# Attention's filler held behind marks of three engines, w_out's loads ordered behind the old sums' loads, heads written in their gate's place

## The chip, the cores and the metric

The kernel runs on one core of one Trainium2 chip. The metric is the device time of one execution in microseconds (us), and lower is better. The core has four compute engines, each with its own queue of instructions: TensorE (PE, matmuls), VectorE (DVE), ScalarE (ACT) and GpSimd (POOL). SyncE (SP) computes nothing here: it issues nearly all DMA transfers, one behind the other. An engine that waits holds up everything behind the waiting instruction in its queue, and that holds for SP too.

## The reference, cut to what matters

One layer of a hybrid decoder: one projection, three groups of heads (attention, a state-space mixer, a gated recurrence), a gate on each, and one output projection. The change touches the attention and the output projection alone.

```
def fox_attention(q, k, v, log_f, q_g, k_g):          # 8 heads x 64, 2048 tokens, causal
    q = rms_norm(q, q_g);  k = rms_norm(k, k_g)
    c = jnp.cumsum(log_f.astype(jnp.float32), axis=1)
    ...
        logits = jnp.einsum('bhqd,bhkd->bhqk', q_i, kt) * scale + (c_i[..., :, None] - ck[:, :, None, :])
        logits = jnp.where(kpos[None, :] <= qpos[:, None], logits, -jnp.inf)
        p = jax.nn.softmax(logits.astype(jnp.float32), axis=-1)
        return jnp.einsum('bhqk,bhkd->bhqd', p, vt)

        y_att = fox_attention(...) * jax.nn.silu(z_att)
        ...
        mix = jnp.concatenate([y_att, y_ssd, y_lru], axis=-1)      # 512 + 1024 + 512 columns
        h = h + jnp.einsum('bse,ed->bsd', mix, w_out[l])           # w_out is 2048 x 1024
```

## The kernel before, in words

**Stages.** Projections, the state-space mixer and the recurrence take the time up to 1267 us, attention the stretch from 1267 to 1866 us, and a tail of output projection alone the rest, up to 2023 us. The order of the instructions on every engine is fixed when the program is built: a scheduler takes the instructions as the code gives them, and places them by its own estimate of when each is ready. What runs on the chip is that order, with waits where one engine needs another's result.

**Attention.** There are 64 units, eight heads by eight blocks of 256 queries, numbered j; a unit has one to eight tasks (j, kp), each of 256 keys, 288 tasks in all and 36 in a head. A task is a score (`score`: four matmuls at L1006 and L1007 into the PSUM tile T), two exponentials on ACT (L1017 writes ph, the high part, and L1018 overwrites T), a subtraction on DVE (L1019, pl, the low part), a sum of rows on POOL (L1028 and L1031), and three tasks later the product with v (`av`, L1061 and L1063, into the tile O). `maxima` prepares the unit that comes next: its row maxima (L965 on PE, L970 to L975 on DVE), and the loads of queries (`load_q`, L820 to L822), of the gate `za` (L950), and at each head's middle unit of the next head's keys and values (`load_head`, L805 to L809). `finish` ends a unit: ACT copies half of O into `to` (L1075), DVE adds the other parts (L1077, L1078), POOL multiplies by za into `to` (L1079), and SP stores `to` in DRAM (L1085).

**The filler.** Between the tasks stands the output projection, which needs nothing of attention until its last quarter. `sweeps` is a generator that goes over w_out's sixteen blocks of 128 rows in four sweeps of four: rows 12 to 15, then 8 to 11, then 4 to 7 and 0 to 3 mixed. Its partial sums go through DRAM between sweeps (`pt_d`: loads `xr` at L1179 and `xo` at L1215, stores at L1190). Each half tile takes twelve matmuls (L1139 to L1141) and two additions on DVE. A sweep needs the next one's eight blocks of w_out in two parts: `load_wo` loads a block as `wor` (SP, L840), and splits it into `woh` (ACT, L854 or L858) and `wol` (DVE, L855 or L859). A load is issued one block ahead of the split that needs it, and there are eight splits for each sweep. `mix` loads the inputs of a tile (`mt`) and makes their high part `mh` on ACT (L1126) and low part `ml` on POOL (L1127).

**What sets the filler's place.** `fill` runs after each task and takes the filler one step on. Its `issue_after` adds a rule to what the step issues: an instruction *on the mark's engine* must stand behind the mark, with no wait on the chip. The mark before is one score matmul, LAG = 4 tasks back, so that only the filler's PE instructions are held. Its ACT, DVE, POOL and SP instructions stand wherever the scheduler's estimate puts them.

Of the kernel before, what the change touches and what calls it, by code (L numbers as in the profile page):

```python
# [18 lines left out]
P = 128  # L19
# [16 lines left out]
LAG = 4  # L36
# [14 lines left out]
def hybrid_block(ctx, tc, x, norm_g, w_in, q_norm_g, k_norm_g, forget_b, ssd_conv_w, ssd_conv_b,  # L51
# [772 lines left out]

    def load_wo(ws, k0, half, last):
        pl = [(k0 + i, n) for i in range(4) for n in range(2)]
        tags = [f"u{p}{half}_{k}" for k in range(KD) for p in "hl"]
        raw = {}  # L830

        def load(j):
            k, n = pl[j]
            if j + 1 < len(pl):
                raw[j] = [upa.tile([P, 512], F32, name=f"wor{k}_{n}", tag=tags[2 * j + 3])]
            else:
                raw[j] = last(f"wor{k}_{n}")
            m = 512 // len(raw[j])
            for i, r in enumerate(raw[j]):
                dma(r, w_out[k * P:(k + 1) * P, n * 512 + i * m:n * 512 + (i + 1) * m])  # L840

        load(0)
        yield
        for j, (k, n) in enumerate(pl):
            if j + 1 < len(pl):
                load(j + 1)
            h = upa.tile([P, 512], F32R, name=f"woh{k}_{n}", tag=tags[2 * j])
            l = upa.tile([P, 512], F32R, name=f"wol{k}_{n}", tag=tags[2 * j + 1])
            m = 512 // len(raw[j])
            for i, r in enumerate(raw[j]):  # L850
                hc, lc = h[:, i * m:(i + 1) * m], l[:, i * m:(i + 1) * m]
                if 4 <= k < 12:
                    g = c1("sg", k - 4)
                    A.activation(hc, r, AF.Copy, scale=g)  # L854
                    V.scalar_tensor_tensor(lc, r, g, hc.bitcast(F32), op0=ALU.mult,  # L855
                                           op1=ALU.subtract)
                else:
                    A.copy(hc, r)  # L858
                    V.tensor_tensor(lc, r, hc.bitcast(F32), op=ALU.subtract)  # L859
            ws[k, n] = (h, l)  # L860
            yield
# [72 lines left out]
        G.memset(mz, 0.0)  # L934
    U = [{} for _ in units]

    def maxima(j):


# [4 lines left out]
        def first():  # L944
            if j % 2 and j + 1 < len(units):
                load_q(j + 1)
            za = a4.tile([64, 256], F32, name=f"za{j}", tag="za")
            u["za"] = za
            p, b = divmod(h, 2)
            dma(za, za_d[p][b * 64:b * 64 + 64, sb * 256:(sb + 1) * 256])  # L950
            if j % 8 == 4 and h < 7:
                load_head(h + 1)
# [39 lines left out]
    def score(j, kp):  # L992
# [21 lines left out]
                flip(j + 1, pt[:, 384:512])  # L1014
        ph = a5.tile([P, 512], F32R, name=f"ph{j}_{kp}", tag="ph")
        pl = a5.tile([P, 512], F32R, name=f"pl{j}_{kp}", tag="pl")
        A.activation(ph[:, 0:n], pt[:, 0:n], AF.Exp, scale=-1.0)  # L1017
        A.activation(pt[:, 0:n], pt[:, 0:n], AF.Exp, scale=-1.0)  # L1018
        V.tensor_tensor(pl[:, 0:n], pt[:, 0:n], ph[:, 0:n].bitcast(F32), op=ALU.subtract)  # L1019
        u[kp] = ph, pl  # L1020

        e = ph.bitcast(F32)
# [43 lines left out]
    def finish(j):  # L1066
# [3 lines left out]
        po = u["O"]  # L1070
        T.matmul(po[0:65, 256:512], onr, u["ah"], start=False, stop=False, skip_group_check=True)
        T.matmul(po[0:65, 256:512], onr, u["al"], start=False, stop=True, skip_group_check=True)
        to = a3.tile([64, 256], F32, name=f"to{j}", tag="to")
        su = a3.tile([1, 256], F32, name=f"su{j}", tag="su")
        A.copy(to, po[64:128, 0:256])  # L1075
        A.copy(su, po[64:65, 256:512])
        V.tensor_tensor(to, po[0:64, 0:256], to, op=ALU.add)  # L1077
        V.tensor_tensor(to, po[0:64, 256:512], to, op=ALU.add)  # L1078
        G.tensor_tensor(to, to, u["za"], op=ALU.mult)  # L1079
        p, b = divmod(h, 2)  # L1080
        cs = slice(sb * 256, (sb + 1) * 256)
        qt = slice(sb * 2, sb * 2 + 2)

        def store():
            dma(at_d[p][b * 64:b * 64 + 64, cs], to)  # L1085
            dma(s_d[qt, h:h + 1, :].rearrange("i o t -> o i t"),
                su.rearrange("o (i t) -> o i t", i=2))
            if h < 7:
                return

            sr = a1.tile([16, P], F32, name=f"sr{j}", tag="sr")
            dma(sr, s_d[qt].rearrange("i h t -> (i h) t"))
            V.reciprocal(sr, sr)
            dma(r_d[qt].rearrange("i h t -> (i h) t"), sr)
            later(lambda: ready.add(sb), 4)
# [71 lines left out]
    def wo_last(nm):  # L1167
        return [o4.tile([P, 512], F32, name=nm, tag="xr")]

    def sweeps():  # L1170
        for i in range(2):
            more = load_wo(ws[i + 1], SEQ[i + 1][0], 1 - i, wo_last)
            xrs = {}

            def load_xr(j):
                t, n = divmod(j, 2)
                if t < NT:
                    xrs[j] = o4.tile([P, 512], F32, name=f"xr{t}_{n}_{i}", tag="xr")
                    dma(xrs[j], (pt_d if i else xf)[t * P:(t + 1) * P, n * 512:n * 512 + 512])  # L1179

            load_xr(0)
            cur = mix(0, *SEQ[i])
# [16 lines left out]
            for _ in more:  # L1199
                pass  # L1200

        more = load_wo(ws[3], SEQ[3][0], 1, wo_last)
        xs = {}
        work = [(t, 2) for t in range(LEAD)]
        for t in range(NT):
# [5 lines left out]
        for w, (t, i) in enumerate(work):  # L1211
            tsl = slice(t * P, (t + 1) * P)
            if i == 2:
                xs[t] = o3.tile([P, D], F32, name=f"xo{t}", tag="xo")
                dma(xs[t], pt_d[tsl, :])  # L1215
            if i == 3 and cur is None:
                while t // 2 not in ready:
                    yield True
# [21 lines left out]
                next(filler)  # L1240
        flip(0, psS.tile([P, P], F32, name="pm0", tag="S"))
    count = [0, FIRST]
    recent = []

    def fill(ins):
        count[0] += 1
        recent.append(ins)
        want = FIRST + count[0] * RATE // 288 + MORE * max(0, count[0] - 288 + END)
        while want > count[1]:
            with tc.issue_after(recent[max(0, len(recent) - 1 - LAG)].ins):  # L1250
                if next(filler):
                    break
            count[1] += 1
# [60 lines left out]
```

## Time and profile before

| | |
|---|---|
| runs | 2018.38, 2027.57 and 2033.65 us, median 2027.57 |
| the profiled execution: its own time | 2024.83 us |
| its span, from the first to the last instruction | 2023.1 us |
| mean granted clock of TensorE | 0.99 |
| PE busy in the span | 1953.6 us (97%) |
| DVE, ACT, POOL busy in the span | 1302.0, 1005.7 and 803.6 us |

How to read it: PE is busy nearly all the time, so a change to the work of the other engines can shorten the time only by PE's idle stretches and by the time that PE runs at half its clock. A row of a timeline gives the start, the duration, the engine, the line, the operation with out<-in, and in brackets the idle time of that engine ahead of it and what ended it. PEclk is the granted clock as a share of 2.4 GHz; 0.50 is 1.2 GHz.

### The profile page before, as it was taken

How to read it: one execution, taken by the hardware profiler on the slowest of the kernel's cores; microseconds unless marked ns; L12 is line 12 of the kernel's file. 1: busy time of each engine (PE TensorE's matmuls, PEld its weight loads, DVE VectorE, ACT ScalarE, POOL GpSimd, SP SyncE). 2: the span in 40 equal slices, each digit the busy share in tenths (PEclk: the TensorE clock that was granted, in tenths of full speed). 3: DMA queues.
4: the chain of work that ended last, by engine and by line, in shares of the span. 5: the costliest groups of instructions: out<-in, count | busy, mean ns of one | idle time of the engine just before them, and what ended most of it. 6: DMA issues, size and time to landing. Idle time of an engine off the chain costs nothing.

```text
span 2023.1 us, 34947 instructions
## 1 busy us (share of the span) xinstructions
PE 1953.6 (97%) x11941; PEld 1708.9 (84%) x11941; DVE 1302.0 (64%) x2573; ACT 1005.7 (50%) x2174; POOL 803.6 (40%) x920
## 2 busy tenths in 40 slices
PE   7999999999999999989999999999999999998899
PEld 6898888898989899778887897888888988887787
DVE  6748555574645556768577535678778887887333
ACT  6624444453544444544444333576766776765010
POOL 0100000232222324444564201687878887876110
PEclk9999999999999999999999999999999999999999
DMA  5332223121212145667666725664663664704453
GB/s 190 82 100 65 70 74 105 47 64 43 70 37 74 32 120 148 183 170 204 211 187 177 192 80 182 189 182 127 186 180 121 181 170 126 217 28 131 125 172 125
DMA packets 260034, 261.32 MB, mean 129 GB/s; under 512 B 26724, under 2 KB 198016, under 8 KB 258304
## 3 DMA queue, kind: packets, MB, share of 16 engines
q1 hardware_dynamic: 259696, 259.05, 43.7%
q8 instruction: 95, 1.56, 0.3%
q0 software_dynamic: 160, 0.03, 0.1%
q14 instruction: 83, 0.68, 0.1%
HBM read 164.22 MB, written 94.77 MB: 128 GB/s over the span
## 4 chain that ended last, share of the span: by engine, by line
PE 42%; DMA 6%; DVE 3%; ACT 2%; issue 2%; POOL 1%; SPq 0%; DVEq 0%; POOLq 0%; ACTq 0%
PE po L1139 5%; PE po L1140 5%; PE po L1141 5%; PE T L1006 3%; PE T L1007 3%; PE O L1061 3%; PE S L965 3%; PE O L1063 2%; DMA ab<-acs_d 2%; PE pza L360 1%; PE pza L361 1%; PE pza L359 1%; PE py L698 1%; PE pqk L347 1%; PE pqk L343 1%
## 5 line engine op out<-in xcount | busy, mean ns | idle before, releaser
L1139 PE MATMUL po<-woh,mh 128*128 128x512 f32 x512 | 204.9, 400 | 11.9 <-DVE xo L1145 7.6
L1019 DVE TENSOR_TENSOR pl<-T,ph 128x512 fp32r<-128x512 f32 (+1 forms) x288 | 187.2, 654 | 45.3 <-ACT T L1018 43.4
L1140 PE MATMUL po<-wol,mh 128*128 128x512 f32 x512 | 202.2, 395 | 0.0
L1141 PE MATMUL po<-woh,ml 128*128 128x512 f32 x512 | 201.4, 395 | 0.0
L1017 ACT ACTIVATE ph<-T 128x512 fp32r<-128x512 f32 (+1 forms) x288 | 165.2, 574 | 55.7 <-PE T L1007 49.9
L1031 POOL TENSOR_TENSOR ac<-ac,ph 128x512 f32<-128x512 f32 x120 | 155.6, 1296 | 29.7 <-ACT ph L1017 24.2
L1018 ACT ACTIVATE T<-T 128x512 f32<-128x512 f32 (+1 forms) x288 | 164.7, 572 | 0.1
L359 PE MATMUL pxx<-uh,wh 128*128 128x512 f32 x384 | 153.3, 401 | 2.2 <-ACT uh L304 2.1
L1006 PE MATMUL T<-q,k 128*128 128x256 f32 x576 | 148.0, 281 | 6.1 <-DVE pl L1019 2.6
L360 PE MATMUL pxx<-ul,wh 128*128 128x512 f32 x384 | 153.7, 401 | 0.0
L1061 PE MATMUL O<-ph,vv 128*128 128x256 f32 (+1 forms) x576 | 149.5, 279 | 3.5 <-DVE to L1078 2.9
L361 PE MATMUL pxx<-uh,wl 128*128 128x512 f32 x384 | 151.2, 396 | 0.0
L347 PE MATMUL pqk<-wh,ul 128*128 128x256 f32 x512 | 150.9, 295 | 0.0
L343 PE MATMUL pqk<-wh,uh 128*128 128x256 f32 x512 | 148.4, 290 | 0.0
L345 PE MATMUL pqk<-wl,uh 128*128 128x256 f32 x512 | 148.3, 290 | 0.0
L420 DVE SCALAR_TENSOR_TENSOR accx<-rtx,cv,accx 128x512 f32<-128x512 f32 x144 | 108.1, 752 | 59.3 <-ACT accx L417 56.3
L1007 PE MATMUL T<-qx,kx 128*128 128x256 f32 x576 | 144.4, 282 | 0.0
L345 PE MATMUL pzs<-wl,uh 128*128 128x256 f32 x512 | 143.7, 281 | 0.0
L347 PE MATMUL pzs<-wh,ul 128*128 128x256 f32 x512 | 143.3, 280 | 0.0
L1063 PE MATMUL O<-pl,vv 128*65 128x256 f32 x576 | 143.2, 280 | 0.0
L343 PE MATMUL pzs<-wh,uh 128*128 128x256 f32 x512 | 143.0, 281 | 0.0
L975 DVE TENSOR_REDUCE mc<-S 128x1 f32<-128x512 f32 x192 | 128.8, 682 | 21.2 <-PE S L965 19.3
(357 smaller groups left out, 5702.3 us busy)
## 6 DMA issues: line engine op xcount, KB each, us to landing
ab<-acs_d SPq DMA_DIRECT2D x64, 256.0 KB
pt_d<-xr SPq DMA_DIRECT2D x64, 256.0 KB
wr<-in_w_in_dram SPq DMA_DIRECT2D x112, 128.0 KB
xt<-in_x_dram SPq DMA_DIRECT2D x16, 512.0 KB
xs_d<-stx SPq DMA_DIRECT2D x32, 256.0 KB
v_d<-vs SPq DMA_DIRECT2D x32, 256.0 KB
wr<-in_w_in_dram SPq DMA_DIRECT2D x128, 64.0 KB
zs_d<-zs SPq DMA_DIRECT2D x32, 256.0 KB
```

What stands on the lines that cost most here:

```text
L343: T.matmul(ps[:, i, :], h[k][:, sl], wh[k], start=(k == 0 and i == 0), stop=False, skip_group_check=True)
L345: T.matmul(ps[:, i, :], h[k][:, sl], wl[k], start=False, stop=False, skip_group_check=True)
L347: ins = T.matmul(ps[:, i, :], l[k][:, sl], wh[k], start=False, stop=last, skip_group_check=True)
L360: T.matmul(ps, wh[k][:, ms], ul[tb][k], start=False, stop=False)
L1006: T.matmul(ps, k2[:, ks], q3[:, qs], start=(jj == 0), stop=False, skip_group_check=True)
L1007: ins = T.matmul(ps, kx[:, ks], qx[:, qs], start=False, stop=True, skip_group_check=True)
L1019: V.tensor_tensor(pl[:, 0:n], pt[:, 0:n], ph[:, 0:n].bitcast(F32), op=ALU.subtract)
L1061: T.matmul(po[:, qs], vv[:, kt, 0:128], ph[:, cs], start=(kt == 0), stop=(kt == 2 * sb + 1), skip_group_check=True)
L1063: T.matmul(po[0:65, q2], vv[:, kt, 64:129], pl[:, cs], start=False, stop=False, skip_group_check=True)
L1139: T.matmul(ps, mh[:, j, :], h, start=(j == 0), stop=False)
L1140: T.matmul(ps, mh[:, j, :], l, start=False, stop=False)
L1141: T.matmul(ps, ml[:, j, :], h, start=False, stop=(j == 3))
```

## The change

Three edits, all in attention and its filler.

1. **Marks of three engines.** `score` notes the exponential of each task (ACT, L1017) and the subtraction (DVE, L1019); `fill` notes the score matmul as before. Each filler step is held behind all three, four tasks back. The filler's ACT and DVE instructions are held now as its matmuls were. POOL and SP are not.
2. **w_out's loads.** `load_wo` gets a list of the loads of the old sums, `loads`; each load of a block of w_out for sweeps 1, 2 and 3 is ordered on SP's queue behind the last load of old sums known when it is issued (order only, no wait).
3. **The heads' place.** The product with the gate is written into `za` itself, not into `to`, and stored from there. `za` has five buffers (four before), `to` two (three before). So the load of za(j+5) overwrites what the store of unit j reads, and has to wait for that store's landing; before, the load of za(j+4) had to wait only for POOL's product of unit j. `to` is free once POOL has read it; before, only once its store had landed.

```
-    def load_wo(ws, k0, half, last):
+    def load_wo(ws, k0, half, last, behind=()):
...
-                dma(r, w_out[k * P:(k + 1) * P, n * 512 + i * m:n * 512 + (i + 1) * m])
+                put = dma(r, w_out[k * P:(k + 1) * P, n * 512 + i * m:n * 512 + (i + 1) * m])
+                if behind:
+                    tc.add_manual_dep(put.ins, behind[-1].ins.name, mybir.DependencyInfo(
+                        mybir.DependencyClass.NoSync, mybir.DependencyReason.DATA))
...
+    marks = {"P": [], "A": [], "V": []}
...
-            za = a4.tile([64, 256], F32, name=f"za{j}", tag="za")
+            za = a5.tile([64, 256], F32, name=f"za{j}", tag="za")
...
-        A.activation(ph[:, 0:n], pt[:, 0:n], AF.Exp, scale=-1.0)
+        marks["A"].append(A.activation(ph[:, 0:n], pt[:, 0:n], AF.Exp, scale=-1.0))
...
-        V.tensor_tensor(pl[:, 0:n], pt[:, 0:n], ph[:, 0:n].bitcast(F32), op=ALU.subtract)
+        marks["V"].append(V.tensor_tensor(pl[:, 0:n], pt[:, 0:n], ph[:, 0:n].bitcast(F32),
+                                          op=ALU.subtract))
...
-        to = a3.tile([64, 256], F32, name=f"to{j}", tag="to")
+        to = a2.tile([64, 256], F32, name=f"to{j}", tag="to")
...
-        G.tensor_tensor(to, to, u["za"], op=ALU.mult)
+        G.tensor_tensor(u["za"], to, u["za"], op=ALU.mult)
...
-            dma(at_d[p][b * 64:b * 64 + 64, cs], to)
+            dma(at_d[p][b * 64:b * 64 + 64, cs], u["za"])
...
-            more = load_wo(ws[i + 1], SEQ[i + 1][0], 1 - i, wo_last)
+            more = load_wo(ws[i + 1], SEQ[i + 1][0], 1 - i, wo_last, loads)
...
-                    dma(xrs[j], (pt_d if i else xf)[t * P:(t + 1) * P, n * 512:n * 512 + 512])
+                    loads.append(dma(xrs[j], (pt_d if i else xf)[
+                        t * P:(t + 1) * P, n * 512:n * 512 + 512]))
...
-        more = load_wo(ws[3], SEQ[3][0], 1, wo_last)
+        more = load_wo(ws[3], SEQ[3][0], 1, wo_last, loads)
...
-                dma(xs[t], pt_d[tsl, :])
+                loads.append(dma(xs[t], pt_d[tsl, :]))
...
-    recent = []
...
-        recent.append(ins)
+        marks["P"].append(ins)
...
-            with tc.issue_after(recent[max(0, len(recent) - 1 - LAG)].ins):
+            with ExitStack() as behind:
+                for m in marks.values():
+                    behind.enter_context(tc.issue_after(m[max(0, len(m) - 1 - LAG)].ins))
```

**Where the splits stand.** Counted by exponentials of attention (288 in all) that stand ahead of a split on ACT: sweep 1's blocks 8_0 to 11_0 stood ahead of attention, all seven, and stand now behind 5, 13, 21, 29, 37, 45 and 53 of them; 11_1 behind 48, now 61. Sweep 2's blocks 4_0 to 7_0 stood behind 114 to 117, and stand now one by one behind 133, 140, 148, 156, 164, 172 and 180; 7_1 behind 175, now 188. Sweep 3's eight stood behind 237 to 242, and stand now behind 244 to 260. The splits on DVE move in the same way. In all, 17 of the 24 stood in attention; now 24 do. On SP's queue, the load of each block of sweep 1 from 9_1 on and of sweep 2 stands now behind the store of a unit whose last task lies 16 to 26 tasks ahead of the split (a unit's result is stored some five tasks after its last); for 4_0 to 7_0 that was 8 to 16 tasks before.

ACT's queue around the first split of sweep 2, before; woh4_0 is the high part of w_out's block of rows 4, first half of the columns, ph27_0 the exponential of unit 27's first task, su25 the copy at unit 25's end.

```order
L1076 COPY su25_17210<-O25_17128 1x256
L854 ACTIVATE woh4_0_17873<-wor4_0_17659,cv_113 128x512
L1017 ACTIVATE ph27_0_17192<-T27_0_17187 128x512
L1018 ACTIVATE T27_0_17187<-T27_0_17187 128x512
L854 ACTIVATE woh4_1_18087<-wor4_1_17871,cv_113 128x512
L1017 ACTIVATE ph27_1_17226<-T27_1_17221 128x512
L1018 ACTIVATE T27_1_17221<-T27_1_17221 128x512
L854 ACTIVATE woh5_0_18388<-wor5_0_18085,cv_113 128x512
L854 ACTIVATE woh5_1_18642<-wor5_1_18386,cv_113 128x512
L854 ACTIVATE woh6_0_18875<-wor6_0_18640,cv_113 128x512
```

ACT's queue of the changed kernel where woh4_0 stands now, in unit 30:

```order
L1022 ACTIVATE ph30_3_17739<-T30_3_17734 128x512
L1023 ACTIVATE T30_3_17734<-T30_3_17734 128x512
L857 ACTIVATE woh4_0_17873<-wor4_0_17659,cv_113 128x512
L1022 ACTIVATE ph30_4_17785<-T30_4_17780 128x512
L1023 ACTIVATE T30_4_17780<-T30_4_17780 128x512
```

The row of splits between unit 25's end and unit 27's tasks is gone; each has exponentials ahead of it and behind it.

SP's queue at the load of head 5's keys, before (to30 is unit 30's result, za34 the gate of unit 34, q30 and qx0 two units' queries in one of three pairs of buffers, k21 the keys), and behind it the same place of the changed kernel:

```order
L1179 DMA xr5_0_1_18392<-pt_d_13455 128x512
L1085 DMA at_d_97<-to30_17940 64x256
L950 DMA za34_18024<-za_d2_79 64x256
L820 DMA q30_9573<-qh_d2_62 64x512
L821 DMA qx0_9576<-qh_d2_62 64x512
L822 DMA qx0_9576<-ql_d2_66 64x512
L805 DMA k21_13440<-kh_d2_70 64x2048
```

```order
L1091 DMA at_d_97<-za30_17395 64x256
L1187 DMA xr5_0_1_18392<-pt_d_13455 128x512
L955 DMA za35_18118<-za_d2_79 64x256
L820 DMA q30_9573<-qh_d2_62 64x512
L821 DMA qx0_9576<-qh_d2_62 64x512
L822 DMA qx0_9576<-ql_d2_66 64x512
L805 DMA k21_13440<-kh_d2_70 64x2048
```

The store of unit 30 now stands two rows ahead of the load of za35, which has to wait for its landing, and the queries stand right behind that load. At the other head turns the queries stand ahead of the gate's load, or the store is further ahead.

SP's queue of the changed kernel where sweep 3's blocks are loaded (xr15_1 is the last sum of sweep 1, xo15 the first old sum of the mixed sweeps, wor0_0 the first block):

```order
L1199 DMA pt_d_13455<-xr15_1_1_20996 128x512
L1131 DMA mt13_4_21578<-gt_d0_95 128x4x128
L1092 DMA s_d_93<-su53_21129 2x1x128
L1224 DMA xo15_21226<-pt_d_13455 128x1024
L840 DMA wor0_0_21328<-in_w_out_dram 128x512
```

and ACT's queue where the first of them is split:

```order
L1022 ACTIVATE ph54_6_21194<-T54_6_21185 128x384
L861 CAST woh0_0_21332<-wor0_0_21328 128x512
L1132 CAST mh14_4_21336<-mt14_4_21338 128x512
L1023 ACTIVATE T54_6_21185<-T54_6_21185 128x384
L1022 ACTIVATE ph55_0_21234<-T55_0_21229 128x512
```

Before, wor0_0 was loaded ahead of xo15 and of su53's store, and its split stood five tasks earlier, ahead of unit 54's last exponentials. From unit 63's last task on, the queues of the four compute engines read alike in both kernels.

## Rows read from the trace of the kernel before

**Rows 1.** The page's first part: busy time, share of the span and instructions of each engine.

```profile
span 2023.1 us, 34947 instructions
PE 1953.6 (97%) x11941; PEld 1708.9 (84%) x11941; DVE 1302.0 (64%) x2573; ACT 1005.7 (50%) x2174; POOL 803.6 (40%) x920
```

**Rows 2.** Busy time by stretches: stretch and its length in us, busy time (and instructions) of PE, PE's weight loads, DVE, ACT and POOL, then the granted clock, the DMA share and GB/s. The attention stretch, and four places in it with a lower clock.

```profile
1267.00:1866.00 599.00, 582.29 (x3769) 520.16 (x3769) 477.83 (x1123) 415.38 (x946) 466.78 (x519) 0.99 0.54 152
1511.20:1515.00 3.80, 3.72 (x14) 3.19 (x15) 3.80 (x7) 3.80 (x8) 2.43 (x4) 0.50 0.81 261
1515.00:1519.00 4.00, 4.00 (x20) 3.35 (x19) 4.00 (x9) 3.90 (x10) 3.41 (x4) 0.73 0.70 181
1776.50:1780.00 3.50, 3.50 (x17) 3.21 (x16) 3.50 (x8) 1.19 (x3) 1.29 (x1) 0.51 0.00 0
1827.00:1831.20 4.20, 4.20 (x18) 3.66 (x19) 4.20 (x11) 3.73 (x9) 3.44 (x4) 0.59 0.16 48
```

**Rows 3.** PE's waits in the attention stretch: the line that waited, what ended the wait, us in total, times, the longest.

```profile
PE S L965 <- DVE mc L975: 3.3, 3, 2.5
PE O L1061 <- DVE to L1078: 2.9, 1, 2.9
PE T L1006 <- DVE pl L1019: 2.6, 2, 2.4
```

**Rows 4.** ACT's timeline at the first split of sweep 2.

```profile
1509.15 0.72 ACT L854 ACTIVATE woh<-wor,cv 128x512 fp32r<-128x512 f32 x1 [5.23 <-DMA wor<-in_w_out_dram]
```

**Rows 5.** DVE's timeline at the same place.

```profile
1509.90 0.75 DVE L855 SCALAR_TENSOR_TENSOR wol<-wor,cv,woh 128x512 fp32r<-128x512 f32 x1 [5.39 <-ACT woh L854]
1510.57 0.41 DVE L1078 TENSOR_TENSOR to<-O,to 64x256 f32<-64x256 f32 x1
```

**Rows 6.** PE's timeline at the same place.

```profile
1507.69 0.28 PE L1061 MATMUL O<-ph,vv 128*128 128x256 f32 x1
1511.13 0.55 PE L1061 MATMUL O<-ph,vv 128*128 128x256 f32 x1 [2.92 <-DVE to L1078]
```

**Rows 7.** Where block 11_1 is split: SP's timeline (its load), and ACT's and PE's.

```profile
1370.15 0.34 SPq L840 DMA_DIRECT2D wor<-in_w_out_dram  x1
...
1373.20 0.72 ACT L854 ACTIVATE woh<-wor,cv 128x512 fp32r<-128x512 f32 x1 [3.08 <-DMA wor<-in_w_out_dram]
...
1374.46 0.39 PE L1061 MATMUL O<-ph,vv 128*128 128x256 f32 x1 [0.55 <-ACT ph L1017]
...
1375.52 0.47 PE L1139 MATMUL po<-woh,mh 128*128 128x512 f32 x1 [0.33 <-DVE mz L973]
```

**Rows 8.** DVE's timeline at 1766 to 1776 us, among sweep 3's splits.

```profile
1769.04 0.67 DVE L859 TENSOR_TENSOR wol<-wor,woh 128x512 fp32r<-128x512 f32 x1
...
1772.56 3.09 DVE L859 TENSOR_TENSOR wol<-wor,woh 128x512 fp32r<-128x512 f32 x1
```

**Rows 9.** POOL's timeline at the same place.

```profile
1768.75 1.55 POOL L1035 TENSOR_TENSOR w<-ac 128x256 f32<-128x256 f32 x1
...
1772.11 1.08 POOL L1079 TENSOR_TENSOR to<-to,za 64x256 f32<-64x256 f32 x1
1773.15 1.26 POOL L1028 TENSOR_TENSOR ac<-ph,ph 128x512 f32<-128x512 f32 x1
1774.38 0.71 POOL L1043 TENSOR_TENSOR al<-w,ah 128x256 fp32r<-128x256 f32 x1
```

**Rows 10.** PE's timeline at two later stalls of the stretch.

```profile
1776.17 0.39 PE L1006 MATMUL T<-q,k 128*128 128x256 f32 x1 [2.43 <-DVE pl L1019]
...
1826.86 0.50 PE L965 MATMUL S<-k,q 96*128 96x512 f32 x1 [2.49 <-DVE mc L975]
```

**Rows 11.** The instructions of the two DVE lines of the splits: smallest, median and largest duration in ns, first and last start.

```profile
L855 DVE SCALAR_TENSOR_TENSOR wol<-wor,cv,woh x16: 730/752/1175, 1235.3 to 1632.6; 128x512 fp32r<-128x512 f32 x16
L859 DVE TENSOR_TENSOR wol<-wor,woh x17: 415/692/3087, 1219.8 to 1780.3; 128x512 fp32r<-128x512 f32 x15, 128x256 fp32r<-128x256 f32 x2
```

**Rows 12.** SP's timeline around sweep 3's first loads, and ACT's at the exponential behind which woh0_0 stands now.

```profile
1764.24 1.27 SPq L1215 DMA_DIRECT2D xo<-pt_d  x3
1766.54 0.62 SPq L1086 DMA_DIRECT2D s_d<-su  x1
...
1770.09 0.49 ACT L1017 ACTIVATE ph<-T 128x384 fp32r<-128x384 f32 x1
```

**Rows 13.** SP's timeline at the load of head 5's keys, and PE's first matmul on those queries.

```profile
1567.66 0.48 SPq L1085 DMA_DIRECT2D at_d<-to  x1
1568.20 0.60 SPq L950 DMA_DIRECT2D za<-za_d  x1
1568.85 0.59 SPq L820 DMA_DIRECT2D q<-qh_d  x1
...
1573.00 0.39 PE L965 MATMUL S<-k,q 96*128 96x512 f32 x1
```

**Rows 14.** The same at another load of queries: SP's issue, and PE's first matmul on them.

```profile
1488.90 0.51 SPq L820 DMA_DIRECT2D q<-qh_d  x1
...
1493.41 0.70 PE L965 MATMUL S<-k,q 96*128 96x512 f32 x2 [0.20 <-DMA q<-qh_d]
```

**Rows 15.** SP's timeline where a load of the old sums' buffer (xr) waits for the landing of the store that read it.

```profile
1407.91 0.33 SPq L1190 DMA_DIRECT2D pt_d<-xr  x1
1409.97 0.34 SPq L1179 DMA_DIRECT2D xr<-in_x_dram  x1
```

More of the change, by code (lines that the diff above doesn't have):

```diff
@@ L1168, in wo_last @@
         return [o4.tile([P, 512], F32, name=nm, tag="xr")]
+    loads = []
     def sweeps():
         for i in range(2):
-            more = load_wo(ws[i + 1], SEQ[i + 1][0], 1 - i, wo_last)
+            more = load_wo(ws[i + 1], SEQ[i + 1][0], 1 - i, wo_last, loads)
             xrs = {}
```

## The prediction

> **What bounds the kernel now.** I read four views, from the coarse to the fine. The page's first part shows TensorE (PE) busy for 1953.6 of 2023.1 us, no other engine for more than 64% [rows 1]: the kernel is bound by PE, and the change takes no matmul away. So I look only for PE's idle time, and for time at a lower clock. Next, busy time by stretches: in attention PE works 582.29 of 599.00 us, which leaves 16.7 us idle. The granted clock is 0.99 there, and the loss stands in a few places: 3.80 us at 0.50 and 4.00 us at 0.73 behind 1511.2 (1.9 + 1.1 = 3.0 us lost), 3.50 us at 0.51 behind 1776.5 (1.7 lost), 4.20 us at 0.59 behind 1827 (1.7 lost), 6.4 us in sum [rows 2]. All three follow an idle PE: the clock fell from 2.4 to 1.2 GHz behind idle times of 2.92, 2.43 and 2.49 us [rows 6, 10], and the first matmul of a kind that had taken 0.28 us took 0.55 [rows 6]. So **the most that attention can give back is 16.7 + 6.4 = 23.1 us, 1.1% of the time**. Third, PE's waits: three single waits (2.5 on mc, 2.9 on to, 2.4 on pl) hold 7.8 of the 16.7 us; the rest is small change [rows 3]. Fourth, the timelines of the engines there, which say what was late.
>
> **The change, part by part.** The sum is made against the profiled execution's own 2024.83 us, which is 2.7 us under the median of the runs shown; I add that 2.7 at the end.
>
> *The burst at 1508, removed.* ACT sat 5.23 us until a block of w_out had landed [rows 4]. DVE's split of that block waited 5.39 us for ACT, and the last addition of a unit (L1078), queued behind the split, came 0.75 us later still [rows 5]. PE needed that addition to be done, so that O was free: 2.92 us idle [rows 6], and then 3.0 us lost at the lower clock [rows 2]. The splits stood there because only PE's share of a filler step was held; ACT's and DVE's went where the scheduler thought the load had landed. Now each block has its own place, eight tasks from the next, and its load stands ten tasks or more ahead of the split. A task takes 599.00/288 = 2.1 us, so the load has over 20 us where landing took 3.1 [rows 7]. I take the whole stall off: **−5.9**.
>
> *The wait for 11_1, removed.* Its load was issued at 1370.15, ACT waited for it until 1373.20, and PE lost 0.55 + 0.33 [rows 7]. The split now stands 13 tasks later: **−0.9**.
>
> *Splits that DVE and POOL stretch.* One split took 3.09 us, where the median is 0.69 [rows 8, 11], while POOL had three operations back to back (1.08, 1.26, 0.71) [rows 9]. That held pl by 2.4 us; PE idled for 2.43 [rows 10] and lost 1.7 at the lower clock [rows 2]: 4.1 us for the one case among 17 splits in attention. With 24 there, the same rate gives 24/17 × 4.1 = 5.8, which is +1.7; with one case again it is 0. I take **0**, with −4.1 (none) and +4.1 (two) as the ends. The split at 1769.04 took 0.67 beside a POOL operation of 1.55 [rows 8, 9], so a neighbour on POOL is not enough by itself.
>
> Here the Trainium skill has a rule (SBUF — State Buffer, "SBUF: two separate sides"): a DVE instruction with two inputs in SBUF and a GpSimd instruction that reads SBUF share a pair of ports under an exclusive lock; the one that starts first holds it for its whole instruction, and the other blocks. By it a split that loses should wait for one POOL operation, at most 1.55 us by these rows. The trace agrees that a split can be blocked, and not on the size: 2.4 us were added, across three operations. The rule speaks against the change, since seven more such splits are put where POOL works; by its size, seven times 1.55 is an estimate of 10.9 us more on DVE, which alone would not fill DVE's idle time there.
>
> *Seven splits moved into attention.* They bring 7 × 0.752 = 5.3 us to DVE [rows 11] and 7 × 0.72 = 5.0 to ACT [rows 4]. DVE is busy 477.83 of 599.00 us, ACT 415.38 [rows 2], and PE is three tasks ahead of the use of pl (the product stands three tasks behind the score). That slack hides a split of 0.75 us: **0**, end +5.3, if no cover is left. They leave a stage in which DVE and ACT were not the bound; I give nothing for it.
>
> *w_out's loads behind the old sums' loads, in sweep 3.* wor0_0 now stands behind xo15, and xo15 behind su53's store. Before, that store went out at 1766.54 and the group of xo loads at 1764.24 [rows 12]. In the new order xo15 goes out at about 1766.54 + 0.62 = 1767.2 and wor0_0 at 1767.6; with 3.1 us of landing [rows 7] it is there at about 1770.7. ACT reaches the split behind the exponential at 1770.09 + 0.49 = 1770.6 [rows 12]. So ACT waits 0.1 us, and up to 2.2 if SP is 2.1 us late by one more landing [rows 15]. Behind the split stand the second exponential of that task and the next task; PE has three tasks of products and filler to do meanwhile. I take **+0.5**, ends 0 and 2.2 + 1.7 = 3.9 (a stall and the lower clock behind it). In the other sweeps the order only keeps the loads back, and each still has its ten tasks.
>
> *The heads in z's place.* One queue pays: at head 5's load the gate's load now waits for the landing of unit 30's store, two rows ahead, and the queries stand right behind it. A store takes 2.06 us from its issue until what waits for its landing goes out [rows 15]. Without the wait the gate's load would go out some 0.9 us behind the store (0.48 for the store [rows 13], 0.34 for the load between [rows 15]), so the queries come 1.1 us later. They had 4.15 us (1568.85 to 1573.00), and PE did not wait [rows 13]; at another load PE came 4.51 us behind the issue and still waited 0.20 [rows 14]. So most of the 1.1 us can show: **+0.6**, ends 0 and, if every one of six head turns were late so, 6 × (2.5 + 1.7) = 25. The fewer buffers of `to` cost **0**: a buffer is free once POOL has multiplied, one short operation (1.08 us at the longest here [rows 9]), instead of after a store's landing; the end is +3, one stall like those of rows 3.
>
> *The first inputs of sweep 1* (mh, ml) are no longer made ahead, since ACT's part is held too: **+0.3**, end +2.5, one such stall.
>
> Sum: −5.9 − 0.9 + 0 + 0 + 0.5 + 0.6 + 0 + 0.3 = −5.4, so 2019.4 for an execution like the profiled one, and 2019.4 + 2.7 = **2022 us** for the median.
>
> **The rivals.** *Nothing net.* The burst's stall goes, but waits of the same kind appear at the new places, since 24 splits each hold up exponentials where seven were outside; two stalls of 2.5 idle and 1.7 at the lower clock give back 8.4 of it, more than the 6.8 taken off: about 2028. For it speaks that attention now carries more work beside the same matmuls; against it, that each split is alone.
>
> *Larger gain.* Neither the stretched split (4.1) nor the wait at 1826.86 (2.49 + 1.7 = 4.2) recurs, and half of the other small waits go (16.7 − 2.9 − 0.9 − 2.4 − 2.5 = 8.0, half is 4.0): 2022 − 12.3 = 2009.7. Against it: the wait at 1826.86 stands in a part that the change does not touch.
>
> *Slower, by stretched splits.* Splits now fall at steady places between exponentials, and if those places suit POOL's sums badly, six of 24 stall as the one at 1772.56 did: five more × 4.1 = 20.5, so 2042.7. It decides from two more on (8.2 against 5.4). For it speaks POOL's share, 466.78 of 599.00 us [rows 2]; against it, one in 17 so far.
>
> *Slower, by SP.* Stores' landings hold SP ahead of the queries at six head turns: 2022 − 0.6 + 25 = 2046.6. It decides when queries come about 3 us later per turn. Against it: only one turn has that order.
>
> *No effect.* That the filler is not held at all is excluded by the order of the queues, which shows each split moved.
>
> **How the numbers follow.** Chances: forecast 0.54 (own range 2015 to 2029), nothing net 0.16, larger gain 0.14, slower by splits 0.09, slower by SP 0.07. The range reaches from 2010, the larger gain's own time, to 2036, halfway to the slower cases: it holds the forecast and nothing net (0.70), half of the larger gain (0.07) and the small end of the slower cases (0.03). A measurement of this kernel can tell about 1%, 20 us, from no change. Faster by over 1% means under 2007.3, where only the far end of the larger gain lies: 0.05. Slower by over 1% means above 2047.8: half of the two slower cases, 0.08. Within: 0.87.
>
> **What would show it.** In the changed profile ACT's splits of sweep 2 should stand one by one, with no wait for a block above 1 us; PE's wait of L1061 for `to` should be gone, the granted clock should stay at 1.00 where blocks 4_0 to 7_0 are split, and PE's busy time should be the same but for about 3 us. DVE's median for the splits should stay near 0.7 us; several above 2 us would mean the first slower rival. SP's gate loads should wait on stores in short pieces, and PE's waits for q should stay under 1.5 us; more would mean the second. I am wrong if PE's idle time in attention stays above 16 us, or falls under 8.

## The result, and the profile after

| | before | changed |
|---|---|---|
| runs | 20, median 2020.72 us (2016.42 to 2033.65) | 20, median 2010.3 us (2006.02 to 2020.08) |
| ratio to before | | **0.9947**, 95% interval 0.9933 to 0.9961 |
| span of the profiled execution | 2023.1 us | 2009.5 us |

The change gains 0.53%, about 10.7 us. It is under 1%, and it is twice the sum of the prediction (5.4 us). The median of 2010.3 us lies at the very edge of the predicted range, 2010 to 2036, and outside the forecast's own range, 2015 to 2029; why is told in the section on the prediction. The page of the changed kernel, where the line numbers are up to nine higher:

```profile
span 2009.5 us, 34885 instructions
PE 1946.7 (97%) x11941; PEld 1705.1 (85%) x11941; DVE 1296.2 (65%) x2573; ACT 1005.0 (50%) x2174; POOL 807.9 (40%) x920
```

The counts of instructions on each engine are those of [rows 1]. To see where the time went, both traces are cut at the same instructions: the starts of attention's exponentials number 0, 110, 136, 240, 264 and 287 of 0 to 287. Busy time by stretches before, with the columns of [rows 2]:

```profile
0.00:1267.60 1267.60, 1227.25 (x7553) 1071.91 (x7554) 763.17 (x1315) 574.37 (x1202) 319.88 (x386) 0.99 0.39 117
1267.60:1496.30 228.70, 224.77 (x1461) 200.58 (x1460) 176.19 (x434) 156.34 (x359) 178.59 (x202) 1.00 0.59 164
1496.30:1556.00 59.70, 55.50 (x346) 48.88 (x345) 46.75 (x108) 41.27 (x92) 43.48 (x47) 0.94 0.61 172
1556.00:1762.70 206.70, 205.64 (x1362) 185.07 (x1361) 169.24 (x401) 150.30 (x345) 168.05 (x192) 1.00 0.60 167
1762.70:1813.40 50.70, 47.03 (x291) 41.30 (x290) 44.07 (x88) 31.51 (x70) 37.00 (x35) 0.97 0.16 52
1813.40:1864.30 50.90, 47.05 (x303) 42.21 (x302) 39.61 (x92) 34.42 (x79) 38.74 (x44) 0.97 0.38 115
1864.30:2023.10 158.80, 146.35 (x638) 118.99 (x636) 63.02 (x141) 17.48 (x32) 17.88 (x17) 0.99 0.46 143
```

and of the changed kernel:

```profile
0.00:1263.50 1263.50, 1225.25 (x7553) 1071.21 (x7554) 755.04 (x1308) 570.07 (x1194) 320.66 (x388) 0.99 0.39 116
1263.50:1490.80 227.30, 224.24 (x1465) 200.84 (x1465) 182.57 (x441) 160.02 (x366) 179.40 (x201) 1.00 0.60 171
1490.80:1541.10 50.30, 50.30 (x333) 45.34 (x332) 42.87 (x102) 37.72 (x86) 42.70 (x48) 1.00 0.61 178
1541.10:1747.50 206.40, 204.89 (x1356) 184.55 (x1355) 169.51 (x404) 150.55 (x344) 168.41 (x190) 1.00 0.59 164
1747.50:1796.50 49.00, 48.12 (x309) 42.04 (x307) 45.78 (x94) 34.56 (x77) 40.22 (x37) 1.00 0.31 103
1796.50:1847.90 51.40, 45.39 (x301) 40.62 (x300) 37.33 (x88) 34.65 (x80) 38.49 (x44) 1.00 0.38 112
1847.90:2009.50 161.60, 148.52 (x637) 120.53 (x636) 63.13 (x142) 17.42 (x31) 17.98 (x17) 0.96 0.44 140
```

The third row is the burst of [rows 4 to 6]: 59.70 us have become 50.30, and PE has no idle time left there (50.30 of 50.30) and a clock of 1.00. The fifth row is that of the stretched split [rows 8 to 10]: PE's idle time falls from 3.67 to 0.88 us and the clock is 1.00; it does 18 matmuls more, so that its length falls by 1.7 alone. The last row gives 2.8 us back. The two executions differ by 13.6 us, more than the medians do, and the first row, 4.1 us of that, can't be read as a gain: in the thirteen other traces of this study attention starts between 1257.8 and 1268.8 us, with and without the splits ahead of it. The last 94.6 us ahead of attention, where the seven splits stood, take the same time with and without them (first row before, second changed):

```profile
1173.00:1267.60 94.60, 92.11 (x554) 80.78 (x554) 46.59 (x102) 32.87 (x67) 5.92 (x9) 0.98 0.42 136
1168.90:1263.50 94.60, 92.10 (x555) 80.78 (x554) 41.76 (x95) 28.30 (x59) 6.57 (x11) 0.98 0.37 119
```

DVE has seven instructions less there and PE gains nothing, so what the seven splits leave behind is worth 0, as the prediction had it. The 4.1 us arose ahead of these rows. Up to PE's matmul number 6900 all fourteen traces have the same order of instructions on every engine, and still it starts at 1149.7 to 1159.2 us (1159.2 before, 1155.2 changed).

ACT no longer waits for a block of w_out in attention, but once for 0.3 us; its waits there, with the columns of [rows 3]:

```profile
ACT q L994 <- PE T L993: 70.5, 37, 4.6
ACT ph L1022 <- PE T L1012: 43.5, 56, 2.7
...
ACT woh L861 <- DMA wor<-in_w_out_dram: 0.3, 1, 0.3
```

PE's waits from 1250 to 1866 us, that is to 18 us behind attention's last exponential, show what came in place of those of [rows 3]:

```profile
PE po L1145 <- DVE xo L1151: 9.3, 4, 3.7
PE S L970 <- DVE mc L980: 4.1, 7, 1.6
PE T L1011 <- ACT q L995: 1.6, 4, 0.7
```

The waits for `to` and `pl` are gone. The longest are now waits for the additions of the last sums (xo). [Rows 3] end with attention; to 18 us behind it, the kernel before had such waits too:

```profile
PE po L1139 <- DVE xo L1145: 5.7, 4, 3.3
...
1871.98 0.63 PE L1139 MATMUL po<-woh,mh 128*128 128x512 f32 x1 [3.33 <-DVE xo L1145]
```

So 3.6 us were added. DVE's timeline at the end of attention in the changed kernel:

```profile
1827.20 0.69 DVE L1123 TENSOR_TENSOR mt<-mt,rb 128x512 f32<-128x512 f32 x1 [0.35 <-DMA mt<-at_d]
1829.90 0.88 DVE L1151 SCALAR_TENSOR_TENSOR xo<-po,rsn,xo 128x256 f32<-128x256 f32 x2 [2.00 <-DMA xo<-pt_d]
...
1836.84 0.94 DVE L1099 RECIPROCAL sr<-sr 16x128 f32<-16x128 f32 x1 [4.48 <-DMA sr<-s_d]
1837.71 0.77 DVE L1151 SCALAR_TENSOR_TENSOR xo<-po,rsn,xo 128x256 f32<-128x256 f32 x2
```

and PE's:

```profile
1830.92 0.47 PE L1145 MATMUL po<-woh,mh 128*128 128x512 f32 x1 [2.11 <-DVE xo L1151]
...
1838.62 0.47 PE L1145 MATMUL po<-woh,mh 128*128 128x512 f32 x1 [2.39 <-DVE xo L1151]
...
1856.27 0.77 PE L1145 MATMUL po<-woh,mh 128*128 128x512 f32 x1 [3.71 <-DVE xo L1151]
```

DVE waits for loads (xo, sr), and PE for the additions queued behind them. Counted by matmuls of this line, the stall of 3.71 us stands where the 3.33 was, the one of 2.39 where 1.13 was, and the one of 2.11 is new.

### The profile page after: what moved, and what is told of

Read it like the earlier page. It is cut to its first block, busy times and chain, and to the rows that moved or that the text cites. A ratio compares the mean times of both kernels' runs of the same rounds, so it can differ in the third digit from the quotient of the medians.

```text
span 2009.5 us, 34885 instructions
## 1 busy us (share of the span) xinstructions
PE 1946.7 (97%) x11941; PEld 1705.1 (85%) x11941; DVE 1296.2 (65%) x2573; ACT 1005.0 (50%) x2174; POOL 807.9 (40%) x920
## 4 chain that ended last, share of the span: by engine, by line
PE 44%; DMA 3%; DVE 2%; issue 1%; ACT 1%; POOL 1%; SPq 1%; DVEq 0%; POOLq 0%; ACTq 0%
PE po L1145 6%; PE po L1146 5%; PE po L1147 5%; PE T L1011 3%; PE T L1012 3%; PE O L1067 3%; PE O L1069 3%; PE S L970 3%; PE pza L360 1%; PE pza L361 1%; PE pza L359 1%; PE pqk L345 1%; PE pqk L343 1%; PE pqk L347 1%; DMA ab<-acs_d 1%
## 5 line engine op out<-in xcount | busy, mean ns | idle before, releaser
L1037 POOL TENSOR_TENSOR ac<-ac,ph 128x512 f32<-128x512 f32 x120 | 158.7, 1323 | 23.8 <-ACT ph L1022 18.1
L1023 ACT ACTIVATE T<-T 128x512 f32<-128x512 f32 (+1 forms) x288 | 164.7, 572 | 0.3
```

## The experiments

All ratios are to runs of the kernel before on the same chip, with a 95% interval; 0.001 is 2.0 us. The table at the end has the stretches of every trace.

**One part alone.** e1 has only the first edit (marks), e2 only the second (order of loads), e3 only the third (place):

```
e1:  +    marks = {"P": [], "A": [], "V": []}   ...  for m in marks.values(): ...
e2:  +    tc.add_manual_dep(put.ins, behind[-1].ins.name, ... NoSync ...)
e3:  +    za = a5.tile(...)   to = a2.tile(...)   G.tensor_tensor(u["za"], to, u["za"], ...)
```

> The marks of three engines alone; loads and places as before. Theory A (the time came from the splits of w_out that stood in a burst and now stand one by one): the splits stand where they stand in the changed kernel, so nearly the whole gain, -8 to -12 us against the kernel before, and no idle time of PE above 1 us at the first split of sweep 2. Rival B (the three edits each bring a part): -3 to -6 us. Rival C (the heads in z's place bring it, through shorter waits of SP and POOL): 0 to -2 us.

> The order of w_out's loads behind the old sums' loads alone, no marks on ACT and DVE. The order of the queues shows that this too takes the burst apart: the splits of 4_0 to 7_0 stand behind 117 to 164 exponentials, in place of 114 to 117. Theory A: so it too gains most of it, -6 to -11 us. Rival B: -2 to -5 us. Rival C: 0 to -2 us.

> The heads written in their gate's place alone (five buffers of za, two of to). The burst stays (4_0 to 7_0 behind 115 to 118 exponentials), with the stall of about 3 us behind it. Theory A: within 2 us of the kernel before. Rival B: -2 to -5 us. Rival C: -6 to -11 us. The rival of the prediction in which gate loads hold SP: +2 to +25 us.

Measured: e1 **0.997** (0.9954 to 0.9986), e2 **1.013** (1.0099 to 1.0161), e3 **1.0053** (1.0032 to 1.0074). e1 gains some 6 us, at the end of rival B's span. Theories A, B and C all fail on e2 and e3: two of the edits cost time when they stand alone. e2 did take the burst apart, and its ACT waits tell why it is slower all the same (1267 to 1890 us):

```profile
ACT woh L857 <- DMA wor<-in_w_out_dram: 39.7, 14, 6.2
```

Without a mark the scheduler puts each split where it thinks the load has landed; the loads now go out later, so 14 of the 16 splits on this line are waited for, and the exponentials behind them too. In e3 the burst and the split of 11_1 stand nearly as before, each close behind its load, while SP now waits for stores ahead of the gate's loads (L950), and with it all that is queued there. SP's waits from 1255 to 1860 us:

```profile
SPq L950 <- DMA at_d<-za: 50.3, 41, 3.4
```

and ACT's timeline at the two places:

```profile
1371.62 0.72 ACT L854 ACTIVATE woh<-wor,cv 128x512 fp32r<-128x512 f32 x1 [7.28 <-DMA wor<-in_w_out_dram]
...
1513.43 0.72 ACT L854 ACTIVATE woh<-wor,cv 128x512 fp32r<-128x512 f32 x1 [6.31 <-DMA wor<-in_w_out_dram]
```

Before, the same waits were 3.08 and 5.23 us [rows 4, 7]. e3's stretches of 0 to 110 and 110 to 136 are 5.5 and 4.1 us longer than before. Its 10.7 us lie in the span that the rival *slower, by SP* gave, but it is w_out's blocks that are waited for, not the queries. That SP's waits for the stores make these blocks late fits, and isn't shown. The load of 11_1 goes out 103.7 us behind the first exponential (102.6 before), and that of 4_0 goes out 9.3 us behind exponential 110 (7.7 before), 1.1 and 1.6 us late. A part of the longer wait for 11_1 comes of ACT's queue alone: the split stands one exponential earlier there (47 ahead of it, 48 before), and starts 1.8 us later, not 4.2.

**The marks, sweep by sweep.** e4 holds ACT's and DVE's share for sweep 2's splits alone, e7 for sweep 1's, e8 for sweep 3's (and all that follows); no order of loads, no new place:

```
e4:  for m in marks.values() if 108 <= count[0] <= 200 else (marks["P"],):
e7:  for m in marks.values() if count[0] < 108 else (marks["P"],):
e8:  for m in marks.values() if count[0] > 200 else (marks["P"],):
```

> The marks of ACT and DVE alone and only for the filler's steps behind tasks 108 to 200, which hold sweep 2's splits; sweeps 1's and 3's splits stand as before. If the burst alone carries the gain: -8 to -11 us. By the sum of the prediction (2.9 idle and 3.0 at the lower clock): -5.9 us. If the gain is mostly of the other sweeps' splits: 0 to -3 us.

> The marks of ACT and DVE for the steps behind the first 107 tasks alone: sweep 1's eight splits spread over attention, seven of them moved into it; the burst of sweep 2 stays. By the prediction's sum (the wait for 11_1 gone, -0.9; first inputs not made ahead, +0.3; seven more splits, 0 to +5.3): -1 to +1 us. If splits inside attention cost their time on DVE: +4 to +6. If they take with them a wait that stood ahead of attention: -2 to -5.

> The marks of ACT and DVE for the steps behind tasks from 201 on alone: sweep 3's splits, and all of the filler's additions in the last units. Burst stays. The stretched split (2.43 us idle and the clock behind it, 4.1 us) goes, as in the profile of the marks alone. By the marks' profile, waits of the output tiles for DVE's additions come near the end, 9.3 us against 7.5 with sweep 2's marks alone: net -4 to 0 us. If these waits are the price: +1 to +5 us.

Measured: e4 **0.9961** (0.9946 to 0.9976), -7.9 us; e7 **1.0024** (1.0009 to 1.0038); e8 **1.0011** (0.9996 to 1.0025). So the burst of sweep 2 is the gain of the marks. Sweep 1's spreading costs 5 us by itself, and the cause is open: of the 3.4 us that its one trace loses in 0 to 110, 1.3 are a wait of PE for a load of queries and 1.7 a place at the lower clock, and e1, with the same splits there, shows neither. Sweep 3's removes the stretched split, but gains nothing in sum. The three give -0.9 us in sum, and all the marks together (e1) gave -6.1; each interval is some 3 us wide to either side, so whether the parts add stays open. The stretched split is no matter of chance: it took 3.09 us in the trace before, in e4 and in e7, where sweep 3's order is the old one, and in these two a score of PE waits for pl as long as in [rows 3]. In all other traces no split of sweep 3 took above 1.8 us, and no score waited for pl above 0.8 us (0.3 in the changed kernel, e1, e5, e6, e8 and e9). One of these is e3, where sweep 3's splits stand nearly as before and the heads have their new place. PE's waits in e4:

```profile
PE po L1142 <- DVE xo L1148: 7.5, 5, 2.9
PE S L967 <- DVE mc L977: 5.7, 7, 2.3
PE T L1008 <- DVE pl L1021: 3.0, 3, 2.4
```

**The changed kernel less one part.** e5 drops the order of loads, e6 the new place:

```
e5:  -    tc.add_manual_dep(put.ins, behind[-1].ins.name, ...)
e6:  -    G.tensor_tensor(u["za"], to, u["za"], op=ALU.mult)      (a4 and a3 as before)
     +    G.tensor_tensor(to, to, u["za"], op=ALU.mult)
```

> The changed kernel without the order of w_out's loads: marks of three engines and the heads in their gate's place. Theory D (the order of loads and the new place cost time only where a split waits closely behind its load; with the marks no split does): like the changed kernel within 4 us, -7 to -12 us against the kernel before, and ACT waits for w_out's blocks less than 6 us in attention. Rival E (each edit brings the cost that it showed alone, whatever the marks do): marks -6 and place +11, so +3 to +7 us.

> The changed kernel without the new place of the heads: marks of three engines and the order of w_out's loads. Theory D: like the marks alone or the changed kernel, -5 to -12 us. Rival E: marks -6 and order +26, so +15 to +22 us.

Measured: e5 **0.9947** (0.993 to 0.9965), e6 **0.9973** (0.9961 to 0.9985). Theory D holds: what the two edits cost alone (26 and 11 us) is not paid with the marks. SP waits in the changed kernel longer than in e3, while ACT's waits for w_out's blocks come to 0.3 us:

```profile
SPq L955 <- DMA at_d<-za: 64.5, 43, 3.4
```

With them the order of loads does nothing that these runs can tell (e5 measures as the changed kernel, e6 as e1), and the new place gains about 5 us, in both pairs (e5 against e6, the changed kernel against e1). By the table, the larger part of it lies in the tail (158.7 against 163.8 us, and 161.6 against 164.7), one execution of each.

**Where the new place gains.** In e1 ACT waits 9.0 us, in four waits, for the landing of heads' stores before it may write `to` again:

```profile
ACT to L1078 <- DMA at_d<-to: 9.0, 4, 3.7
```

e9 takes these waits from e1 in another way:

```
-        to = a3.tile([64, 256], F32, ...)
-        su = a3.tile([1, 256], F32, ...)
+        ts = a5.tile([65, 256], F32, name=f"to{j}", tag="to")
+        to, su = ts[0:64, :], ts[64:65, :]
```

> The marks alone, the heads written as before into to, but to has five buffers instead of three (su becomes a 65th row of it, which frees the space). No order of loads, no new place. Theory F (with marks, the new place gains about 5 us because ACT no longer waits for the landing of the heads' stores before it may write to: 9.0 us of such waits with the marks alone): these waits go, and so the gain of the marks with the new place, -9 to -12 us. Rival G (the new place gains through POOL's or SP's order): like the marks alone, -4 to -7 us, with ACT's waits gone all the same.

Measured: **0.9972** (0.9959 to 0.9984), like e1: theory F falls by its own number, and rival G's number holds; in its trace ACT's waits for `to` are gone. That POOL's or SP's order is the reason, as G has it, isn't shown. The trace is more divided. The stretches up to 240 are as short as in the changed kernel (e1's 208.2 us for 136 to 240 become 206.6), and the end of the kernel is longer by as much (166.7 us, against 164.7 in e1 and 161.6).

**The end.** e10 drops the marks of ACT and DVE behind task 200 of the changed kernel, e11 holds the reciprocal back, e12 gives `sr` three buffers (with e9's joint tile, four buffers, for space):

```
e10: for m in marks.values() if count[0] <= 200 else (marks["P"],):
e11: -            V.reciprocal(sr, sr)
     -            dma(r_d[...], sr)
     +            def invert():
     +                with tc.issue_after(marks["V"][-1].ins):
     +                    V.reciprocal(sr, sr)
     +                dma(r_d[...], sr)
     +            later(invert, 2)
e12: -            sr = a1.tile(...)
     +            sr = a3.tile(...)
```

> The changed kernel with the marks of ACT and DVE dropped for the steps behind tasks above 200: sweep 3's splits stand in groups of four behind 243 and 246 exponentials (the order of loads holds them there), and the filler's additions in the last units are free. If the marks near the end cost what they gain (+1 us measured by themselves): like the changed kernel, -9 to -12 us. If the waits of output tiles for DVE's additions near the end are their doing: -12 to -16. If the groups of four stall as the burst did: -3 to -7.

> The changed kernel, and in the last head the reciprocal of the sums (DVE) is issued two tasks later and held behind the newest subtraction, so that its load has landed: in the changed kernel DVE waited 8.8 us for these loads in three waits, with additions of output tiles behind them that PE waited for. If these waits are on the path: 3 to 6 us faster than the changed kernel, -13 to -17 against the kernel before. If DVE then waits for the old sums' loads in their place: within 2 us of the changed kernel.

> The changed kernel with three buffers instead of one for the reciprocals of the sums (sr) in the last head; su becomes a 65th row of to (four buffers of both), which frees the space. In the changed kernel the loads of sr62 and sr63 wait on SP for the landing of the store before them, and the tail's first loads (mt11, xo10) are queued behind: PE stood 11.4 us for additions of output tiles from the last units on, and the stretch from unit 60 to the end takes 3.6 us longer than before the change. Theory H (this chain on SP gives back part of the gain): the tail is 3 to 6 us shorter than the changed kernel's, -13 to -17 us against the kernel before. Rival I (the tail's first stalls come from the output stores that free the buffers of old sums): within 2 us of the changed kernel, -9 to -12.

Measured: e10 **0.9971** (0.9954 to 0.9988), e11 **0.9963** (0.9949 to 0.9978), e12 **0.9954** (0.9941 to 0.9968). None beats the changed kernel. In e10 the order of loads holds the splits in groups of four, and the stretch 240 to 264 takes 54.1 us against 49.0 (50.6 before), so there the marks are worth their place, as long as the order of loads stands beside them. e11 gains 5.3 us in 264 to 287 and loses 7.6 in the tail. In e12 the reciprocals of the last three units come without a long wait, but DVE stands for the loads of the tail as long as before, as rival I had it:

```profile
1875.26 0.69 DVE L1123 TENSOR_TENSOR mt<-mt,rb 128x512 f32<-128x512 f32 x1 [4.33 <-DMA mt<-at_d]
```

Stretches between the same exponentials in each trace (one execution each), in us; the last ends with the span:

| | ahead | 0-110 | 110-136 | 136-240 | 240-264 | 264-287 | tail |
|---|---|---|---|---|---|---|---|
| before | 1267.6 | 228.7 | 59.8 | 206.7 | 50.6 | 51.0 | 158.8 |
| changed | 1263.5 | 227.3 | 50.3 | 206.4 | 49.0 | 51.4 | 161.6 |
| e1 marks | 1262.4 | 228.9 | 50.6 | 208.2 | 48.5 | 49.5 | 164.7 |
| e2 order | 1268.8 | 239.9 | 59.6 | 210.7 | 55.0 | 51.2 | 159.8 |
| e3 place | 1264.2 | 234.2 | 63.9 | 207.9 | 46.4 | 52.5 | 159.6 |
| e4 sweep 2 | 1263.3 | 227.3 | 51.2 | 209.1 | 49.8 | 50.8 | 158.5 |
| e5 no order | 1259.6 | 227.4 | 50.3 | 206.4 | 48.5 | 51.4 | 158.7 |
| e6 no place | 1259.8 | 228.6 | 50.6 | 207.2 | 48.7 | 49.8 | 163.8 |
| e7 sweep 1 | 1257.8 | 232.1 | 59.4 | 206.8 | 50.7 | 50.7 | 162.6 |
| e8 sweep 3 | 1262.8 | 227.8 | 59.9 | 205.8 | 48.5 | 48.8 | 161.1 |
| e9 five to | 1264.5 | 228.0 | 50.4 | 206.6 | 48.5 | 48.6 | 166.7 |
| e10 | 1262.1 | 227.2 | 50.3 | 206.2 | 54.1 | 50.9 | 161.1 |
| e11 | 1262.0 | 227.4 | 50.3 | 206.4 | 48.6 | 46.1 | 169.2 |
| e12 | 1259.5 | 227.8 | 50.5 | 206.4 | 50.7 | 54.9 | 161.3 |

## Why the prediction was right, and where its sizes were off

The mechanism was right: the burst's stall goes, and it is the largest term. The sizes were off, and that 2010.3 us falls into the range, by 0.3 us, is luck: it stands 11.7 us under the forecast and beside the time of the rival *larger gain* (2009.7). Of the 11.7 us, 6.9 come of the three runs before, whose median was that much above the 20 of the result; a gain of 10.7 us from their 2027.57 would be 2016.8, inside the forecast's own range. By the gain itself the result lies between the forecast's 5.4 and the rival's 17.7 us, a little nearer to the forecast. Of that rival's parts, the stretched split went, and no wait for mc above 1.6 us is left where there had been 2.49; the stalls of 2.11 and 2.39 us that came at the additions (1.13 before) took a part of it back. The times given for the two slower rivals, 2042.7 and 2046.6, are 0.1 to 0.2 us above their own sums; nothing hangs on it.

Of the signs named ahead, PE's idle time in attention came out inside its bounds of 8 and 16 us: 16.7 became 11.5 (rows two to six of the stretches). PE's busy time there fell by 7.0 us, from 580.0 to 572.9, where about 3 was said, because all three places at the lower clock went and not the burst's alone.

The steps, one by one:

- **The burst, -5.9.** Too small. In its stretch PE lost 59.70 - 55.50 = 4.2 us idle and 0.06 × 59.70 = 3.6 at the lower clock, 7.8 in all, and all of it went; e4, which does this alone, measured -7.9 us, in an interval (-10.9 to -4.9) that holds 5.9 too. The step had taken one stall (2.92) and left out the smaller ones near it.
- **The wait for 11_1, -0.9, and sweep 1's first inputs, +0.3.** The stretch 0 to 110 is 1.4 us shorter in the changed kernel. That fits, but e4, with sweep 1's old order, is as short there (227.3), e1 with the new one is not (228.9), and e7, with the same splits, measured +5: these terms are not shown, and the seven splits moved in are not proved free, only free in the company of the rest.
- **The stretched split, 0.** This failed, because it was priced as a rate (one in 17). The order on every engine is fixed, and the meeting of split and POOL recurred where the order there stayed (e4, e7) and was gone where it moved. Its 4.1 us went, though e8, which removes it alone, measured no gain. The splits in attention are stretched more often, without a wait of a score for pl: 10 of 24 took above 1 us, before 5 of 17, and they take 24.8 us of DVE in sum, before 17.0, so 7.8 more where the prediction said 5.3. Of 16 on this line the median is 902 ns and the largest 1826, before 752 and 1175 [rows 11]:

```profile
L858 DVE SCALAR_TENSOR_TENSOR wol<-wor,cv,woh x16: 732/902/1826, 1271.2 to 1645.6; 128x512 fp32r<-128x512 f32 x16
```

- **wor0_0, +0.5.** ACT waits 0.3 us (above), close to the 0.1 that was reckoned, and no wait of PE above 0.6 us stands near it.
- **The heads' place, +0.6.** The order was read rightly: the gate's load goes out 2.21 us behind the store, where it had been 0.54 [rows 13], and the queries 2.76 us behind the store, where it had been 1.19:

```profile
1551.92 0.48 SPq L1091 DMA_DIRECT2D at_d<-za  x1
1552.51 0.52 SPq L1187 DMA_DIRECT2D xr<-pt_d  x1
1554.13 0.46 SPq L955 DMA_DIRECT2D za<-za_d  x1
1554.68 0.55 SPq L820 DMA_DIRECT2D q<-qh_d  x1
```

  PE first used them at 1561.50, with no wait, so it cost nothing here. The sign of the whole edit was wrong: alone it costs 11 us, with longer waits for w_out's blocks, but with the marks, as in the changed kernel, it gains 5. The prediction looked at who waits for `za` and for the queries, and not at ACT's waits for the stores that freed `to`, which the edit takes away.
- **The tail, nothing.** The queues read alike there, and it is 2.8 us longer: 0.6 us more idle, the rest longer busy at a lower clock (0.96 against 0.99). In e5, which measures the same, it is 158.7 us as before, so one execution doesn't tell whether the change lengthens it. The rival *nothing net* awaited new stalls at the splits; those that came stand at the additions.
- **From execution to median, +2.7.** The median of three runs was high. By 20 runs the profiled execution lay 4.1 us above the median, so the same sum would have given 2024.8 - 5.4 - 4.1 = 2015.3.

Left open: why the new place gains with the marks (ACT's waits may explain the stretches up to 240, but e9, without them, lost as much at the end), and what sets the tail's length. It went from 158.5 to 169.2 us in these traces, and what e11 and e12 took from one wait there came back as another.

## What to carry to other kernels

A filler held on one engine alone still runs ahead on the others, and its loads are waited for by whatever stands behind them in the same queue: hold every engine whose queue the main work shares. The cost of an edit that delays a shared DMA queue can depend on who waits closely behind a load: here the same edit cost 11 us before the splits were moved away from their loads, and gained 5 after. Where the order is fixed when the program is built, a stall between two engines can be a property of that order and not a rate, as the split that took 3.09 us in three executions: ask whether the order around it moves. Not all of the time is so fixed: with one and the same order, the first 6900 matmuls took 1149.7 to 1159.2 us.

## What the runs showed that had not been expected

In the changed kernel stalls of PE of 2.11 and 2.39 us left the clock at 1.00. The one of 3.71 us was followed by 1.2 GHz, and so was one of 2.12 us in the tail; before, 2.43 us was enough [rows 2, 10]. The fourth stall, and a window of the changed kernel at each:

```profile
1877.85 0.47 PE L1145 MATMUL po<-woh,mh 128*128 128x512 f32 x1 [2.12 <-DVE xo L1151]
...
1830.00:1836.00 6.00, 5.08 (x33) 4.62 (x33) 2.32 (x7) 2.62 (x6) 3.18 (x4) 1.00 0.36 102
1838.60:1844.60 6.00, 5.98 (x37) 5.31 (x38) 2.95 (x7) 2.47 (x7) 2.99 (x5) 1.00 0.31 89
1854.40:1861.20 6.80, 4.93 (x12) 3.80 (x12) 2.42 (x5) 0.00 (x0) 0.72 (x1) 0.50 0.20 55
1878.30:1881.60 3.30, 3.30 (x10) 2.53 (x9) 0.07 (x1) 0.00 (x0) 0.00 (x0) 0.50 0.30 107
```

So a stall is not a sure price of 1.7 us more, as the prediction had it, and its length alone doesn't tell the price: of these four, two cost only themselves. By estimate, the last cost some 1.7 us more (half of the 3.30), and the one of 3.71 some 2.5 (half of the 4.93 us that PE was busy at 0.50).
